# A hybrid diffusion layer on Trainium2: the two latent FFNs done in two phases, gate and up by seven products of half blocks

## The chip, the cores and the metric

The kernel runs on one core of one Trainium2 chip, as one program. The metric is the device time of one execution in microseconds (us). The engines work side by side, each on its own queue in order: TensorE (PE in the rows) multiplies, VectorE (DVE), ScalarE (ACT) and GpSimd (POOL) do the rest, and SyncE (SP) issues nearly all transfers between DRAM and SBUF.

## What is computed

One layer over 1024 latent tokens of width 1024 and 256 context tokens: a half-step FFN, a mixing sublayer, a second half-step FFN. The FFNs of the latent tokens are what changes:

```python
def rms_norm(x, g):
    return x * lax.rsqrt(jnp.mean(x * x, axis=-1, keepdims=True) + EPS) * g
def macaron_ffn(x, mod3, norm_pre, norm_post, w_gate, w_up, w_down):
    h = modulate(rms_norm(x, norm_pre), mod3[:, 0], mod3[:, 1])     # h * (1 + scale) + shift
    y = (jax.nn.silu(h @ w_gate) * (h @ w_up)) @ w_down             # 1024 -> 2816 -> 1024
    return x + 0.5 * mod3[:, 2] * rms_norm(y, norm_post)
...
mod = silu(c) @ ada_w + ada_b        # nine vectors of 1024: shift, scale, gate of each sublayer
h @ w_in  ->  u_f, z, x|B|C, dt      # mixing: Fourier group and a two-way SSD scan, then w_out
```

## The kernel before

Matrix products run in a 32-bit format that keeps part of a float32's digits, so each operand is split into a high and a low part (`split`, L182: ScalarE casts, VectorE subtracts) and each product is three matmuls (`mm3`, L398: high by high, high by low, low by high), 128 rows deep and at most 512 columns wide.

The hidden width 2816 is 22 tiles f of 128, taken in pairs j. `ffn_x` (L467) goes through the eleven pairs: gate and up of two tiles over all tokens (`g1_pair`, 8 row blocks x 2 chunks of 512 tokens x 3 matmuls, that is 48 for gate and 48 for up of a tile), then down (`g2`): for each of the 8 token tiles 12 matmuls into PSUM, which VectorE adds to the tile's y in SBUF (L465). With the last pair each token tile goes on to `post`: the norm of y, gate and residual (`post_norm`, L611), x1 written to DRAM, and the norm and the transposes (`ptr`, L642) of the next sublayer. In TensorE's queue the first products of the next sublayer (`pch`) stand among these. FFN1 begins with the first half of the tokens while the second half of x is loaded.

The modulations that FFN1 does not need itself are 14 units (`ada_units`, L541; a unit is half a vector): four loads of 512 KB (`adaR`), two steps on VectorE for each (L561, L563; twice as many where the context has the vector too), then a product with a matrix of ones (`pmod`) and a turn of the result. All 14 run beside FFN1, with a ring of three buffers.

`project` (L730) then does the channels of the Fourier group and C (`pch`, 256 columns), convolutions over the tokens (`conv`), the tokens' z and dt (`pz`), and the other channels (`pch`, 512 columns, 285 matmuls before anything else comes between). SBUF is cut by hand into regions (R, X, F); PSUM is cut anew for each stage. Which instruction comes when in a queue is set when the program is built; the queues are then fixed.

Of the kernel before, what the change touches and what calls it, by code (L numbers as in the profile page):

```python
# [26 lines left out]
R_WORDS, X_WORDS, F_WORDS = 20992, 13824, 18300  # L27

# columns of the per-partition vector table
# [6 lines left out]
# columns of the constant table  # L36
# [4 lines left out]
class Bank:  # L41
    """One SBUF tile cut by hand: an area is free again for what is traced after its release."""

    def __init__(self, pool, n, dtype, name):
        self.t = pool.tile([128, n], dtype, name=name)
        self.name = name
        self.view = {dtype: self.t}
        other = F32 if dtype is FR else FR
        self.view[other] = self.t.bitcast(other)
        self.holes = [(0, n)]  # L50


class Mem:
    """float32 areas and areas of float32r operands: a tile holds one kind only"""
# [67 lines left out]
class Kernel:  # L122
    def __init__(self, tc, a, out, st, dbg):
# [4 lines left out]
        self.xpool = None  # L128
# [3 lines left out]
        self.rs = self.nc.gpsimd  # the engine of the small steps of the norms  # L132
# [4 lines left out]
        self.swap(FR)  # L137

    def swap(self, kind):
        """the exchange region begins anew, with areas of one kind"""  # L140
        if self.xpool is not None:
            old = next(k for k, b in self.m.banks.items() if self.X in b)
            assert self.X.holes == [(0, X_WORDS)], self.X.holes
            self.m.banks[old].remove(self.X)
            self.xpool.close()
        self.xpool = self.st.enter_context(contextlib.ExitStack())
        self.nx = getattr(self, "nx", 0) + 1
        pool = self.xpool.enter_context(self.tc.tile_pool(name=f"x{self.nx}", bufs=1, reuse_waits="tile"))
        self.X = Bank(pool, X_WORDS, kind, f"X{self.nx}")
        self.m.banks[kind].append(self.X)  # L150

# [30 lines left out]
    def split(self, hi, lo, src, n, off=0, soff=None, E=None):  # L182
        """src (float32 area) into float32r parts hi + lo, exactly."""
# [47 lines left out]
    def run(self):  # L231
        m = self.m
        self.setup()
        self.banks(main=2, AUX=4)
# [7 lines left out]
    def setup(self):  # L242
# [5 lines left out]
        self.AB = m.alloc(8 * 2 * 5)  # (vector, shift|scale, d tile)  # L248
# [3 lines left out]
        self.cvec = m.alloc(16)  # L252
        self.ccols = m.alloc(256)
        self.G_d = self.dram([4, 1024], "G_d")

    def start(self):
        """norm of x, the shift and scale of its first sublayer, h^T."""
        m, nc, a = self.m, self.nc, self.a
        V, S = nc.vector, nc.scalar
        self.hh = [m.alloc(4096, FR, self.R0) for _ in range(2)]  # L260
        self.hl = [m.alloc(4096, FR, self.R0) for _ in range(2)]
        ada = Ring(m, 2048, 2)
        adaw = []

        def ada_load(j):
            if j < 8:
                adaw.append(ada.next())
                self.load(adaw[j], a["ada01"][j])

        xt = [m.alloc(1024) for _ in range(8)]  # L270
        junk = m.alloc(1024, FR, self.X)

        def xload(t):
            self.load(xt[t], a["x"][t * 128 : t * 128 + 128, :])
# [3 lines left out]
        xload(0)  # L278
        xload(1)
        self.load(self.pvt, a["pv"])  # L280
        ada_load(0)
        xload(2)
        xload(3)
        self.wrings(2, 3, self.X)
        self.raw.i = 0
        w1 = a["ffn1_w1"]
        self.wfirst = [self.weights(w1[0])]
        self.load(self.ct, a["consts"][:, :C_ID], 0, C_ID)
        ada_load(1)
        self.wfirst.append(self.weights(w1[1]))  # L290
        # silu(c), silu(c_ctx) as two columns of a 32-wide stationary operand
# [6 lines left out]
        V.tensor_copy(out=m.r(self.tri_r, 0, 256), in_=m.f(self.ct, C_TGT, C_TGT + 256))  # L298
        V.tensor_tensor(out=m.r(self.tri_r, 256, 384), in0=self.cst(C_TLE), in1=self.cst(C_TGT), op=ALU.add)

        full = Ring(m, 512, 2)
        ssm = m.alloc(256, top=True)

        def xnorm(t):
            ss = self.tmp(1)
            self.sumsq(m.f(xt[t]), ss, junk)
            self.rs = V if t < 4 and t % 2 == 0 else nc.gpsimd
            r = self.rstd(ss, 1, 1.0 / D)
            V.tensor_scalar(out=m.f(xt[t]), in0=m.f(xt[t]), scalar1=r, scalar2=None, op0=ALU.mult)

        def mods(j):
            w = adaw[j]
            P = self.psum("pada", "AUX")
# [4 lines left out]
            ada_load(j + 2)  # L318
# [9 lines left out]
        def hT(c, k):  # L328
            P = self.psum("ptr", "AUX")
            for t in range(4):  # L330
                nc.tensor.transpose(out=P[:, 128 * t : 128 * t + 128], in_=m.f(xt[4 * c + t], 128 * k, 128 * k + 128), identity=self.ident())
            f = full.next()
            if c and k % 2:
                S.activation(out=m.f(f), in_=P, func=AF.Identity, scale=self.A(0, k), bias=self.B(0, k))
            else:
                V.tensor_scalar(out=m.f(f), in0=P, scalar1=self.A(0, k), scalar2=self.B(0, k), op0=ALU.mult, op1=ALU.add)
            self.split(self.hh[c], self.hl[c], f, 512, k * 512, 0)

        for t in range(4):
            xnorm(t)  # L340
        P = [self.psum("gu"), self.psum("gu")]
        self.gfirst = P
        for j in range(8):
            mods(j)
            if 2 <= j < 6:
                # not before the loads that are needed sooner
                V.tensor_copy(out=m.f(xt[j + 2], 0, 1), in_=self.A(0, j))
                xload(j + 2)
                xnorm(j + 2)
            hT(0, j)  # L350
            for i in range(2):
                self.g_half_k(P[i], self.wfirst[i], (self.hh, self.hl, 512), 0, j)

        ada.release()
        self.yfirst = [m.alloc(1024) for _ in range(4)]

        def second():
            """the second half of the tokens, once the first has begun"""
            for k in range(8):
                hT(1, k)  # L360
            m.free(*xt, ssm, junk, self.ccols, self.cvec)
            self.banks(main=3, aux=1)
            full.release()
            self.raw.areas.append(m.alloc(1024, F32, self.F0))

        self.second = second

    # index of a vector: 0 x ffn1, 1 ctx ffn1, 2 x mix, 3 ctx mix, 4 x ffn2
# [29 lines left out]
    def mm3(self, outs, lh, ll, rh, rl, first, last):  # L398
        """outs[c] += (lh + ll)^T (rh[c] + rl[c]) but for the product of the two low parts"""
        n = len(outs)  # L400
        for ps, (l, r) in enumerate(((lh, rh), (lh, rl), (ll, rh))):
            for c in range(n):
                self.nc.tensor.matmul(out=outs[c], lhsT=l, rhs=r[c], start=first and ps == 0, stop=last and ps == 2)  # L403
# [11 lines left out]
    def g1_pair(self, w, hT, g):  # L415
        m, nc = self.m, self.nc
        P = self.psum("gate")
        self.g_half(P, [P[:, 0:512], P[:, 512:1024]], w, 0, hT, (0, 1))
        s = self.sg.next()
        nc.scalar.activation(out=m.f(s), in_=P, func=AF.Silu)  # L420
        P = self.psum("up")
        self.g_half(P, [P[:, 0:512], P[:, 512:1024]], w, 1, hT, (0, 1))
        nc.vector.tensor_tensor(out=m.f(s), in0=P, in1=m.f(s), op=ALU.mult)  # L423
        self.split(g[0], g[1], s, 1024)
# [13 lines left out]
    def g1_one(self, w, hT, g, c, P=None, off=0, n=None):  # L438
        """one chunk of at most 512 tokens, or n of it: gate and up in one PSUM tile"""
# [27 lines left out]
    def ffn_x(self, name, hT, y, post, step=lambda: None, first=None, gu=None, begun=lambda: None, tail=lambda i: None, ending=lambda: None):  # L467
        """all tokens; the first and the last two tiles of d_ff take the two halves of the tokens in turn.
# [11 lines left out]
        for j in range(NG):  # L480
# [10 lines left out]
            if last:  # L491
                ending()
# [1027 lines left out]
```

## Time and profile before

| what | value |
|---|---|
| median of 3 runs (lowest, highest) | 2373.26 us (2372.77, 2375.87) |
| the profiled execution, its span | 2374.1 us |
| TensorE busy | 2241.8 us, 94% |
| VectorE, ScalarE, GpSimd busy | 1230.7, 735.0, 438.6 us |
| FFN1 with the start, to the first z product | 0 to 868.4 us |
| project, context and mixing | 868.4 to 1628.2 us |
| FFN2 | 1628.2 to 2374.1 us |

The stages are read from the timeline of TensorE by the names of its products. A busy share is an average; where TensorE waits is read from the timeline and from the chain of waits.

### The profile page before, as it was taken

What the parts mean: (1) busy time and instruction counts of PE and PEld (TensorE: products, weight loads), DVE (VectorE), ACT (ScalarE), POOL (GpSimd) and SP (SyncE); (2) the same over time, 40 slices, a digit from 0 to 9 for tenths busy, and PEclk for the clock granted to TensorE, in tenths of its full rate; (3) what the DMA queues carried; (4) which work ended last, traced back from release to release, by engine and by line L of the source; (5) the groups of instructions that cost most, each with busy time, mean ns of one, the idle gap of its engine ahead of it and who ended that gap; (6) DMA issues with size and microseconds to landing.
All of it is one profiled execution on the core that took longest, in us unless ns stands there. A gap on an engine that the chain in (4) does not pass through costs nothing. (4 is left out here: it accounts for less than half of the span.)

```text
span 2374.1 us, 27935 instructions
## 1 busy us (share of the span) xinstructions
PE 2241.8 (94%) x11228; PEld 1898.4 (80%) x11228; DVE 1230.7 (52%) x1785; ACT 735.0 (31%) x1141; POOL 438.6 (18%) x490
## 2 busy tenths in 40 slices
PE   7999999999999999988989987898999999999997
PEld 4788888888888899877888866676888888888886
DVE  5744456555534732357888857785233332333335
ACT  3411111111113742336555554455311111111112
POOL 2000000000002500027775722662000000000005
PEclk9999999999999999998999989989999999999999
DMA  7322223333321421123445354333111111111104
GB/s 291 117 82 86 63 88 107 107 114 102 96 71 63 168 88 60 45 62 107 142 143 172 109 185 138 133 127 133 62 45 48 42 54 54 45 54 45 54 9 142
DMA packets 69009, 228.67 MB, mean 96 GB/s; under 512 B 8064, under 2 KB 13824, under 8 KB 67856
## 3 DMA queue, kind: packets, MB, share of 16 engines
q1 hardware_dynamic: 68880, 226.89, 29.3%
q8 instruction: 88, 1.44, 0.2%
q14 instruction: 41, 0.34, 0.0%
HBM read 200.37 MB, written 26.49 MB: 96 GB/s over the span
## 5 line engine op out<-in xcount | busy, mean ns | idle before, releaser
L403 PE MATMUL y<-X,R 128*128 128x512 f32 x2112 | 493.4, 391 | 6.6 <-ACT R L186 3.5
L403 PEld LDWEIGHTS y<-X,R 128*128 128x128 f32 x2112 | 396.1, 188 | 93.0 <-DVE F L465 5.9
L186 ACT CAST X<-F 128x1024 fp32r<-128x1024 f32 (+2 forms) x151 | 157.0, 1041 | 907.3 <-PE up L403 316.5
L403 PE MATMUL up<-R,X 128*128 128x512 f32 x1728 | 397.8, 389 | 0.0
L403 PE MATMUL gate<-R,X 128*128 128x512 f32 x1728 | 397.7, 389 | 0.0
L403 PEld LDWEIGHTS up<-R,X 128*128 128x128 f32 x1728 | 324.4, 188 | 67.3
L403 PEld LDWEIGHTS gate<-R,X 128*128 128x128 f32 x1728 | 324.4, 188 | 67.3
L187 DVE TENSOR_TENSOR X<-F,X 128x1024 fp32r<-128x1024 f32 (+2 forms) x150 | 183.6, 1226 | 300.4 <-ACT X L186 278.8
L195 POOL TENSOR_SCALAR F<-F 128x1 f32<-128x1 f32 x24 | 6.6, 275 | 1419.6 <-ACT F L216 1376.8
L465 DVE TENSOR_TENSOR F<-y,F 128x1024 f32<-128x1024 f32 x160 | 191.6, 1219 | 111.7 <-PE y L403 111.2
L187 DVE TENSOR_TENSOR R<-F,R 128x1024 fp32r<-128x1024 f32 (+3 forms) x167 | 190.0, 1141 | 99.5 <-ACT R L186 93.2
L186 ACT CAST R<-F 128x1024 fp32r<-128x1024 f32 (+4 forms) x184 | 159.0, 872 | 187.3 <-PE pch L403 48.1
L423 DVE TENSOR_TENSOR F<-up,F 128x1024 f32<-128x1024 f32 x36 | 44.1, 1225 | 299.6 <-PE up L403 299.6
L403 PE MATMUL gu<-R,X 128*128 128x512 f32 (+1 forms) x960 | 189.9, 355 | 5.0 <-DVE R L187 3.1
L403 PEld LDWEIGHTS gu<-R,X 128*128 128x128 f32 x960 | 156.6, 192 | 31.6 <-DVE R L187 5.3
L403 PE MATMUL pch<-R 128*128 128x512 f32 (+1 forms) x720 | 145.4, 360 | 7.6 <-DVE F L727 6.2
L403 PE MATMUL gu<-R 128*128 128x256 f32 x1056 | 142.8, 295 | 7.5 <-DVE X L465 6.2
L403 PEld LDWEIGHTS gu<-R 128*128 128x128 f32 x1056 | 135.8, 199 | 12.7 <-DVE X L465 7.4
L403 PEld LDWEIGHTS pch<-R 128*128 128x128 f32 x720 | 121.5, 193 | 27.7 <-DVE F L727 5.3
L1018 POOL TENSOR_TENSOR R<-F 128x384 fp32r<-128x384 f32 x128 | 128.7, 1033 | 35.4 <-PE pD L1052 20.0
L563 DVE SCALAR_TENSOR_TENSOR F<-F 128x512 f32<-128x512 f32 x140 | 101.5, 747 | 34.5 <-DMA F<-adaR 33.3
L403 PE MATMUL y<-R 128*128 128x512 f32 x264 | 73.0, 421 | 1.9 <-ACT R L186 1.9
(256 smaller groups left out, 2314.8 us busy)
## 6 DMA issues: line engine op xcount, KB each, us to landing
F<-ffn_w SPq DMA_DIRECT2D x132, 512.0 KB
F<-ffn_wd SPq DMA_DIRECT2D x66, 512.0 KB
F<-adaR SPq DMA_DIRECT2D x56, 512.0 KB
F<-w_ch SPq DMA_DIRECT2D x26, 512.0 KB
F<-x SPq DMA_DIRECT2D x16, 512.0 KB
F<-ada SPq DMA_DIRECT2D x8, 1024.0 KB
x_d<-F SPq DMA_DIRECT2D x16, 512.0 KB
F<-x_d SPq DMA_DIRECT2D x16, 512.0 KB
```

Of the source, the lines that this page charges most:

```text
L186: nc.scalar.copy(out=m.r(hi, off, off + n), in_=m.f(src, soff, soff + n))
L187: (E or nc.vector).tensor_tensor(out=m.r(lo, off, off + n), in0=m.f(src, soff, soff + n), in1=m.f(hi, off, off + n), op=ALU.subtract)
L195: V.tensor_scalar(out=mv, in0=ss, scalar1=scale * RSQ_M, scalar2=EPS * RSQ_M, op0=ALU.mult, op1=ALU.add)
L403: self.nc.tensor.matmul(out=outs[c], lhsT=l, rhs=r[c], start=first and ps == 0, stop=last and ps == 2)
L423: nc.vector.tensor_tensor(out=m.f(s), in0=P, in1=m.f(s), op=ALU.mult)
L465: nc.vector.tensor_tensor(out=m.f(y[t]), in0=P, in1=m.f(y[t]), op=ALU.add)
L563: V.scalar_tensor_tensor(out=ac, in0=m.f(w, 512 * i, 512 * i + 512), scalar=m.f(self.sil, 8 * v + k, 8 * v + k + 1), in1=ac, op0=ALU.mult, ...
L1018: G.tensor_tensor(out=m.r(R, 384 * i, 384 * i + 384).rearrange("p (h l) -> p h l", h=3), in0=self.cst(tri).unsqueeze(1).broadcast_to([128, ...
```

## The change

**Phase 1, gate and up.** The four quarters of the product are rows of two halves: two f tiles of a pair (columns of w), two halves of the 1024 rows of w (h), two halves of the tokens. Instead of eight products of quarters seven are done (`PROD`), on sums of quarters of w and of h. A unit u = (j, part) is gate or up of a pair: 7 products x 4 row steps x 3 = 84 matmuls of 512 columns where 96 were. VectorE makes the sums of weights (`usums`), low parts (`usplit`) and combines the results (`u_first`, `u_mid`, `u_late`, `u_end`). Sums of h are made once per FFN, in four steps (`h_sums`, `h_split`; GpSimd takes part of the lows). FFN1 needs all of x for them; FFN2 does its first pair plainly (192 matmuls), and reads h back from DRAM (`h3_d`) for the sums. Rows of g go to DRAM (`g_d`).

**Phase 2, down.** `ffn_down` goes three times over all f, for token tiles (0,1), (2,3,4), (5,6,7); y stays in PSUM. For each pass and f it loads and splits 512 KB of w and 128 or 192 KB of g. `post` takes y from PSUM; in FFN1 it goes through one buffer b.

**Modulations.** Units 0 to 5 stay beside FFN1 (ring of one), 6 to 13 go beside the z products (ring of two, one fp32 `pmod` each).

```diff
+PROD = {1: ("A11", "B11"), 2: ("A12", "B21"), 3: ("S4", "B22"), 4: ("A22", "T4"), 5: ("S1", "T1"), 6: ("S2", "T2"), 7: ("S3", "T3")}
...
+    def h_sums(self, hb):
+        b = [m.f(hb, 512 * q, 512 * q + 512) for q in range(7)]
+        V.tensor_tensor(out=b[4], in0=b[2], in1=b[3], op=ALU.add)
+        V.tensor_tensor(out=b[3], in0=b[3], in1=b[0], op=ALU.subtract)
+        V.scalar_tensor_tensor(out=b[5], in0=b[2], scalar=-1.0, in1=b[3], op0=ALU.mult, op1=ALU.subtract)
+        V.tensor_tensor(out=b[6], in0=b[1], in1=b[5], op=ALU.add)
...
+    def ffn_up(self, begun, step=lambda: None):
+        for u in range(n):
+            if u or not begun:
+                for p in (1, 6):
+                    self.product(u, p)
+            self.u_first(u)
...
+            if u + 1 < n:
+                self.usums(u + 1)
+                self.usplit(u + 1, "A11")
+            step()
+            if u > (1 if begun else 0):
+                self.u_late(u - 1)
+                self.usplit(u, "S4")
+            for p in (5, 7):
+                self.product(u, p)
+            self.u_mid(u)
+            if u + 1 < n:
+                self.usplit(u + 1, "S1")
+                if u + 2 < n:
+                    self.uload(u + 2)
+            step()
+        self.u_late(n - 1)
...
+        def prep(q):
+            p, f = todo[q]
+            t0, n = passes[p][0] * 128, len(passes[p]) * 128
+            w, g = self.wraw.next(), self.graw.next()
+            self.load(w, wd[f // 2][:, f % 2 * 1024 : f % 2 * 1024 + 1024])
+            self.load(g, self.g_d[f][:, t0 : t0 + n], 0, n)
+            wh, wl = self.wring.next()
+            gh, gl = self.gring.next()
+            self.split(gh, gl, g, n)
+            self.split(wh, wl, w, 1024)
...
+        ring, acc, sp = Ring(m, 1024, 1, F32, X2), Ring(m, 512, 2, F32, X2), Ring(m, 1024, 1, FR, X1)
+        st = self.ada_steps(self.ada_units(ring, acc, sp, (V,)), range(6))
+        self.ffn_up(True, lambda: next(st))
...
         zs = Ring(m, 384, 2)
+        ring, ac2 = Ring(m, 1024, 2, F32, self.Q), Ring(m, 512, 2, F32, self.Q)
+        st = self.ada_steps(self.ada_units(ring, ac2, None, (V,), "TR"), range(6, 14))
         for nm, n in (("w_zdt", 408), ("w_z1", 384)):
             for t in range(8):
                 P = self.psum("pz", "PZ")
                 self.tok_proj(P, n, t, sets[nm])
+                for _ in range(3):
+                    next(st)
```

Three places in the queues. First TensorE at the end of FFN1 (y: down, ptr: transposes of the normed tile, pch: first products of project), before:

```order
L403 MATMUL y<-X_65,R_60 128x512
L403 MATMUL pch<-R_60,X_65 128x256 x16
L403 MATMUL y<-X_65,R_60 128x512 x4
L403 MATMUL pch<-R_60,X_65 128x256 x4
L403 MATMUL y<-X_65,R_60 128x512 x14
L403 MATMUL pch<-R_60,X_65 128x256 x3
L642 MATMUL ptr<-F_61 128x128 x4
L403 MATMUL pch<-R_60,X_65 128x256 x4
L642 MATMUL ptr<-F_61 128x128 x4
L403 MATMUL pch<-R_60,X_65 128x256 x69
```

and now:

```order
L461 MATMUL y<-Q1a 128x512 x8
L461 MATMUL y<-Q1a,X3a 128x512 x4
L461 MATMUL y<-Q1a 128x512 x2
L803 MATMUL ptr<-F_61 128x128 x24
L461 MATMUL pch<-R_60 128x256 x48
L461 MATMUL pch<-R_60,X3a 128x256 x96
```

The transposes of three token tiles now stand in one row ahead of every pch. Second, TensorE at the end of the z products (pdec and ptot belong to the decays, pmod to the modulations), before:

```order
L403 MATMUL pz<-X_65,R_60 128x384 x73
L881 MATMUL pdec<-F_61 128x96
L882 MATMUL pdec<-F_61 128x96
L883 MATMUL pdec<-F_61 128x96
L884 MATMUL pdec<-F_61 128x96
L885 MATMUL ptot<-F_61,R_60 128x192
L403 MATMUL pz<-X_65,R_60 128x384 x119
L403 MATMUL pch<-R_60 128x512 x285
```

and now:

```order
L725 MATMUL pmod<-Q4a,R_60 128x512
L461 MATMUL pz<-X3a,R_60 128x384 x80
L725 MATMUL pmod<-Q4a,R_60 128x512
L1082 MATMUL pdec<-Q4a,F_61 128x96
L1083 MATMUL pdec<-Q4a,F_61 128x96
L1084 MATMUL pdec<-Q4a,F_61 128x96
L1085 MATMUL pdec<-Q4a,F_61 128x96
L1086 MATMUL ptot<-Q4a,R_60 128x192
L725 MATMUL pmod<-Q4a,R_60 128x512 x4
L461 MATMUL pch<-R_60 128x512 x285
```

Four products of modulations stand between the last z product and the first pch. Third, SP's queue at the same place, now (z_d: z written out, grows and G_d: the gate rows of units 12 and 13):

```order
L990 DMA z_d<-Q4a 128x384
L184 DMA Q4a<-adaR 128x1024 x11
L736 DMA Q4a<-grows 1x1024
L184 DMA Q4a<-adaR 128x1024
L741 DMA G_d<-Q4a 1x512
L184 DMA Q4a<-adaR 128x1024 x3
L736 DMA Q4a<-grows 1x1024
L741 DMA G_d<-Q4a 1x512
L184 DMA Q4a<-ctx 128x1024 x2
```

Fifteen loads of modulation weights stand behind the last z written out; before, none stood there.

## Rows read from the trace of the kernel before

**Rows 1.** Page: span, and busy time of each engine (share of span, instructions).

```profile
span 2374.1 us, 27935 instructions
...
PE 2241.8 (94%) x11228; PEld 1898.4 (80%) x11228; DVE 1230.7 (52%) x1785; ACT 735.0 (31%) x1141; POOL 438.6 (18%) x490
```

**Rows 2.** Chain of waits in FFN2: start us, us, engine and work.

```profile
1834.64 10.88 PE gate L403 x48
...
1878.16 21.76 PE y L403 x96
```

**Rows 3.** Stretches: busy us of each engine, clock, DMA share, GB/s.

```profile
core 0: us, PE busy (x) PEld busy (x) DVE busy (x) ACT busy (x) POOL busy (x), PEclk, DMA share, GB/s
...
100.00:400.00 300.00, 299.82 (x1320) 247.09 (x1319) 159.86 (x195) 59.04 (x63) 0.00 (x0) 1.00 0.27 84
```

**Rows 4.** TensorE by line up to 89.02 us: busy us, mean ns, idle.

```profile
L403 PE MATMUL gu<-R,X 128*128 128x512 f32 x145 | 41.0, 424 | 5.0 <-DVE R L187 3.1 <-ACT R L186 1.5 <-DVE X L187 0.4
...
L403 PE MATMUL y<-X,R 128*128 128x512 f32 x24 | 6.4, 410 | 0.0
```

**Rows 5.** Timeline of TensorE, end of FFN1's start.

```profile
89.02 11.04 PE L403 MATMUL gu<-R,X 128*128 128x512 f32 x48
```

**Rows 6.** Groups by line and form of VectorE, ScalarE and GpSimd: mean ns of one.

```profile
L187 DVE TENSOR_TENSOR X<-F,X 128x1024 fp32r<-128x1024 f32 x144 | 178.0, 1237 | 276.8 <-ACT X L186 276.4 <-PE gu L403 0.3
...
L563 DVE SCALAR_TENSOR_TENSOR F<-F 128x512 f32<-128x512 f32 x140 | 101.5, 747 | 34.5 <-DMA F<-adaR 33.3
...
L187 DVE TENSOR_TENSOR R<-F,R 128x512 fp32r<-128x512 f32 x28 | 19.7, 712 | 11.3 <-ACT R L186 11.3
...
L186 ACT CAST X<-F 128x1024 fp32r<-128x1024 f32 x145 | 152.0, 1050 | 905.8 <-PE up L403 316.5 <-PE y L403 281.4 <-PE gate L403 266.3
...
L187 POOL TENSOR_TENSOR R<-F,R 128x1024 fp32r<-128x1024 f32 x17 | 43.5, 2562 | 19.8 <-ACT R L186 19.8
```

**Rows 7.** Timeline of VectorE and GpSimd near the end.

```profile
2325.53 1.28 DVE L619 SCALAR_TENSOR_TENSOR F<-F 128x1024 f32<-128x1024 f32 x1 [1.05 <-POOL F L202]
...
2328.80 2.40 POOL L620 TENSOR_TENSOR F<-F 128x1024 f32<-128x1024 f32 x1
...
2328.88 3.40 DVE L619 SCALAR_TENSOR_TENSOR F<-F 128x1024 f32<-128x1024 f32 x1 [2.06 <-POOL F L202]
```

**Rows 8.** Timeline of SP's queue and of VectorE: a load of modulation weights.

```profile
94.73 1.09 SPq L172 DMA_DIRECT2D F<-adaR  x2
...
98.43 1.41 DVE L563 SCALAR_TENSOR_TENSOR F<-F 128x512 f32<-128x512 f32 x2 [2.97 <-DMA F<-adaR]
...
100.90 1.41 DVE L563 SCALAR_TENSOR_TENSOR F<-F 128x512 f32<-128x512 f32 x2
```

**Rows 9.** Timeline of TensorE in project: channel and z products.

```profile
857.80 10.72 PE L403 MATMUL pch<-R,X 128*128 128x256 f32 x88
...
868.36 2.40 PE L403 MATMUL pz<-R 128*128 128x408 f32 x12
...
939.23 64.87 PE L403 MATMUL pch<-R 128*128 128x512 f32 x285 [0.63 <-ACT F L789]
```

**Rows 10.** Timeline of ScalarE: silu of the last convolution.

```profile
880.09 1.06 ACT L728 ACTIVATE F<-F 128x1024 f32<-128x1024 f32 x1 [2.13 <-DVE F L727]
```

**Rows 11.** Timeline of TensorE: start and end of FFN2.

```profile
1628.19 8.10 PE L403 MATMUL gu<-R,X 128*128 128x512 f32 x35
...
1646.47 1.12 PE L642 MATMUL ptr<-F 128*128 128x128 f32 x4 [2.01 <-ACT F L647]
...
1647.24 24.20 PE L403 MATMUL gu<-R,X 128*128 128x512 f32 x96
...
2352.42 8.35 PE L403 MATMUL y<-X,R 128*128 128x512 f32 x36
```

**Rows 12.** Chain of waits: a transfer of 384 KB.

```profile
1485.13 3.65 DMA F<-y_d
```

**Rows 13.** Stretch (busy, clock, DMA) and timeline of TensorE after an idle spell.

```profile
1095.00:1100.00 5.00, 0.18 (x1) 0.50 0.20 50
...
1100.92 3.62 PE L403 MATMUL y<-R 128*128 128x512 f32 x8
```

More of the change, by code (lines that the diff above doesn't have):

```diff
@@ L258, in start @@
         m, nc, a = self.m, self.nc, self.a
[L259 to L274, printed above, removed]
+        V, S, G = nc.vector, nc.scalar, nc.gpsimd
@@ L280, in start @@
         self.load(self.pvt, a["pv"])
         ada_load(0)
[L282 to L288, printed above, removed]
-        ada_load(1)
-        self.wfirst.append(self.weights(w1[1]))
+        for t in range(4, 8):
+            self.load(xt[t], a["x"][t * 128 : t * 128 + 128, :])
+        ada_load(1)
+        self.raw = Ring(m, 2560, 1, F32, self.F0)
@@ L357, in second @@
[L357 to L366, printed above, removed]
+            o = m.f(hb, 512 * slot, 512 * slot + 512)
+            if c:
+                S.activation(out=o, in_=P, func=AF.Identity, scale=self.A(0, k), bias=self.B(0, k))
+            else:
+                V.tensor_scalar(out=o, in0=P, scalar1=self.A(0, k), scalar2=self.B(0, k), op0=ALU.mult, op1=ALU.add)
@@ L402, in mm3 @@
             for c in range(n):
-                self.nc.tensor.matmul(out=outs[c], lhsT=l, rhs=r[c], start=first and ps == 0, stop=last and ps == 2)
+                self.nc.tensor.matmul(out=outs[c], lhsT=l, rhs=r[c], start=first and ps == 0, stop=last and ps == 2, skip_group_check=again)
     def g_half(self, P, outs, w, half, hT, chunks):
@@ L541, in ada_units, with units, uload @@
-    def ada_units(self):
+    def units(self, name, j0):
+        self.uw, self.ulist = self.a[name + "_w1"], [(j, part) for j in range(j0, NG) for part in range(2)]
+        self.uraw, self.P, self.srow, self.U = {}, {}, {}, {}
+    def uload(self, u):
+        j, part = self.ulist[u]
+        m = self.m
+        w = self.uraw[u] = self.raw.next()
+        self.nc.sync.dma_start(out=m.f(w, 0, 2048).rearrange("p (f c) -> p f c", f=2),
+                               in_=self.uw[2 * j : 2 * j + 2, :, 1024 * part : 1024 * part + 1024].rearrange("f p c -> p f c"))
@@ new lines, in u_first, with u_dest @@
+    def u_first(self, u):
+        self.U[u] = self.ut.next()
+        U = self.m.f(self.U[u])
+        self.nc.scalar.copy(out=U, in_=self.P[u, "A"])
+        self.nc.vector.tensor_tensor(out=U, in0=self.P[u, "B"], in1=U, op=ALU.add)
+    def u_dest(self, u):
+        j, part = self.ulist[u]
+        if part == 0 and j not in self.srow:
+            self.srow[j] = (self.sg.next(), self.sg.next())
+        m = self.m
+        s = [m.sub(self.srow[j][q // 2], 512 * (q % 2), 512) for q in range(4)]
+        return s, (s if part == 0 else [None] + self.cc)
@@ new lines, in u_late @@
+    def u_late(self, u):
+        m, nc = self.m, self.nc
+        V = nc.vector
+        j, part = self.ulist[u]
+        s, d = self.u_dest(u)
+        self.product(u, 2)
+        self.u_end(u, 0, s, d)
+        for p, tag, q in ((3, "C", 1), (4, "D", 2)):
+            self.product(u, p)
+            V.tensor_tensor(out=m.f(d[q]), in0=self.P[u, tag], in1=m.f(self.U[u]), op=ALU.add)
+            self.u_end(u, q, s, d)
+        if part:
+            for i in range(2):
+                nc.sync.dma_start(out=self.g_d[2 * j + 1 - i], in_=m.f(self.srow[j][i]))
@@ L597, in unit, with ada_steps @@
                                                op0=ALU.add, op1=ALU.mult)
-        def done():
-            for r in (ring, acc, sp):
-                r.release()
-        return unit, done
+        return unit
+    @staticmethod
+    def ada_steps(unit, us):
+        for u in us:
+            yield from unit(u)
+        while True:
+            yield
     def gload(self, slot):
@@ new lines, in ffn1, with step, post @@
+        self.wch = []
+        def step(p):
+            state["n"] = state.get("n", 0) + 1
+            i = len(self.wch)
+            if p == 2 and i < 6 and state["n"] >= 46 + 3 * i:
+                w, r = state["w"][i], self.wraw.next()
+                self.load(r, a["w_ch"][i])
+                self.split(w[0], w[1], r, 1024)
+                self.wch.append(w)
+        def post(t, P):
+            self.rs = V if t > 5 else nc.gpsimd
+            c = t // 4
+            b, xx = state["b"], x.next()
+            self.post_norm(P, m.f(b), state["G"], xx, a["x"][t * 128 : t * 128 + 128, :], V)
+            nc.sync.dma_start(out=self.x1_d[t], in_=m.f(b))
+            self.pre_norm(m.f(b), 2, m.r(self.hh[c]), m.r(self.hl[c]), 512, (t % 4) * 128, xx, full, "AUX", True, V if t > 6 else None)
@@ new lines, in ffn1, with pairs @@
+        state["b"] = m.alloc(1024, F32, X2)
+        self.ffn_down("ffn1", ((0, 1), (2, 3, 4), (5, 6, 7)), post, step, before)
+        for r in (x, full, self.graw, self.wraw):
+            r.release()
+        m.free(state["G"], state["b"])
+        for r in (self.wring, self.gring):
+            for q in r.areas:
+                m.free(*q)
+    def pairs(self, bank, nw, ng):
+        m = self.m
+        if bank is self.Q:
+            self.wring, self.gring = Pairs(), Pairs()
+        self.wring.areas += [tuple(m.alloc(1024, FR, bank) for _ in range(2)) for _ in range(nw)]
+        self.gring.areas += [tuple(m.alloc(384, FR, bank) for _ in range(2)) for _ in range(ng)]
```

585 lines of the change are left out of this document (368 added, 217 removed).

## The prediction

> **What bounds the kernel now.** I read the busy shares first: TensorE works 2241.8 of 2374.1 us [rows 1], so only work that it loses, or waits that it gains, can change the time. The chain of waits then gives the price of a product: in the FFNs it is nothing but matmuls, 48 in 10.88 us and 96 in 21.76, so a 512-column matmul costs 0.2267 us [rows 2]. The table of stretches shows what stands beside it: in 100:400 TensorE has no gap while VectorE is busy 159.86 of 300 us [rows 3]. VectorE therefore has about 47% to give in the FFNs, no more. The profiled execution (span 2374.1) is 0.8 us above the median of 2373.26, so I sum against 2374.1 and take 0.8 off. Changes within 0.2% (4.7 us) I call the same.
>
> **The change part by part.**
>
> *Fewer products.* Each latent FFN had 22 x (96 + 48) = 3168 matmuls of 512 columns. FFN1 now has 22 units of 84 and 1056 for down = 2904, FFN2 192 plain ones, 20 x 84 and 1056 = 2928. 504 x 0.2267 = -114.3 us, if TensorE never waits: -59.9 and -54.4. The 16 matmuls that the modulations lose in FFN1 are another -3.7.
>
> *Start of FFN1.* At 89.02 us the old kernel had done 144 gate/up and 24 down matmuls [rows 4, 5], worth 38.1 us: 51 us lost. The new one needs all of x, and for each of four steps sums of the quarters of h before its products. For a step VectorE has four sums (0.71 each) and a low part of 2048 (2 x 1.24), together 5.3 us, so 21 us; with the scaling of eight x tiles, eight evictions and modulations, and the sums and lows of the first weights I count some 47 us [rows 6]. GpSimd takes the other lows, four of 1536, 1.5 x 2.56 = 3.84 us each [rows 6]. While it works on SBUF, a VectorE operation with two SBUF inputs stands: the same line took 1.28 us alone and 3.40 beside a GpSimd addition of 2.40 [rows 7]. So 47 + 15 us, from about 18 us on: the last low at 80 us, 39 matmuls before it. That is 74 us lost with a few waits, +23. If the two engines do not meet, +8; if every wait adds, +30.
>
> *FFN1, gate and up.* A unit gives TensorE 19.04 us. VectorE has three sums and three lows of weights, an addition and four combinations, four multiplications more for up: 10.8 us for gate, 13.6 for up [rows 6]. In 16 or so of 22 units a modulation adds up to twelve steps of 0.75 [rows 6], which makes 20 to 22 us; the units between have slack, but not all of it carries over. I take +10, between 0 and +45 (no carry at all).
>
> *Up to down.* The first g rows are loaded only after the last ones have left their buffers. FFN1: two VectorE operations, a write (I take the 3.65 us of a 384 KB transfer [rows 12]), a load, a cast: 10 us idle. FFN2: 6 us. After an idle spell the granted clock read 0.50, and 8 matmuls took 3.62 us where 1.81 is the full rate [rows 13], so 2 to 3 us each time: +12 and +9. Between passes: post runs through one buffer b; I find 5 and 3 us.
>
> *Tail of FFN1.* Ahead, TensorE's queue had the channel products (pch) between y and the transposes; now 24 transposes, those of tiles 5, 6 and 7, stand before the first pch, so all pch wait for tile 7. A turn of b is two passes of 1024 (2 x 1.24), a 512 KB write and the issue, about 7.5 us; two turns and the norm of tile 7 end some 20 us after the last y; with the clock 22. What was lost there before: from 89.02 to the first pz at 868.36 are 779.3 us [rows 5, 9], of which 3000 matmuls take 680, 40 of the modulations 9 and 576 pch at 10.72/88 us 70 [rows 9]. The other 20 are 64 transposes (I take 6) and waits of 14. So +8.
>
> FFN1 together: -59.9 - 3.7 + 23 + 10 + 12 + 5 + 8 = -6.
>
> *Eight modulations beside the z products.* This is where I expect the gain to go. Units 6 to 13 ran under FFN1, where their loads were hidden. Now they share two buffers in project, and their last four products stand in TensorE's queue ahead of 285 pch which need nothing of them. One load of 512 KB: two issued at 94.73, the first used at 98.43, so 3.7 us, then two steps, 1.41 [rows 8]; with 0.2 for the issue a buffer turns in 5.3 us. A unit has four loads on two buffers, 10.6 us, then its fp32 product (between 0.23 and 1 us, I take 0.7) and a turn of the same ring for its result (1.7): 13 us, and units hardly overlap, since the result holds a buffer. Four units also write a row to DRAM before the buffer is free, +2 each. The first load goes out after the last convolution, whose silu ended at 881.15, 12.8 us after the first pz [rows 9, 10]; later ones queue on SP behind the z weights, whose raw buffers now overlap the convolution's input: +5. And pz products themselves wait: z_d writes and pmods are in the same queues, some +6. So 12.8 + 8 x 13 + 8 + 5 + 6 = 136 us from the end of the first pch to the next; it was 939.23 - 868.36 = 70.9 [rows 9]. +65. Lower bound: the loads alone keep both buffers turning, 12.8 + 32 x 5.3 / 2 = 98, +27. Upper: +80.
>
> The load's price has a rule beside it: the Trainium skill (DMA: Bandwidth & Descriptors, Anatomy of one DMA) gives 2.0 us plus bytes at 436 GB/s for a DMA. By that a load is an estimated 3.2 us, 0.5 less than the row, a unit 1.0 less, and the stage some 8 us shorter; it was fitted on another issuing path, and I keep the row.
>
> *FFN2.* 144 plain matmuls cover 33 us after the transposes of tile 7, with the clock 35. Meanwhile h goes to DRAM and comes back for the sums: write 4, two loads in line 8, sums and lows 10, the same again for the other two steps 15, first weights 5, their sum and cast 2.5: 44 us. +10 idle, +12 with the clock (0 to +20). Up to down +9, passes +3. Before, of 2374.1 - 1628 = 746 us the products took 718; 28 were lost, of which 8 at the transposes remain [rows 11]. The last pair's 7 us go, and the end after the last y is some 10.5 instead of 13.3, as no addition to y is left: -9.5. FFN2: -54.4 + 12 + 9 + 3 - 9.5 = -40.
>
> The mixing stages between keep their operations; h goes to DRAM on a queue with room. 0, +-8.
>
> **Sum.** -6 + 65 - 40 = +19; 2374.1 + 19 - 0.8 = 2392. That is slower by 0.8%.
>
> **Rivals.**
> (a) Faster. The modulations stream: if the results turn over while the next loads run, the stage costs the lower bound, +27, and the sum is 2354. For it: VectorE has little else there. Against: a unit's second load waits for the buffer that holds the last result. It decides as soon as a unit takes less than 13 - 19/8, about 10.6 us.
> (b) Slower still: VectorE becomes the bound in FFN1. Each unit with modulation steps then takes the 22 us of its VectorE work, and nothing carries over: +45 instead of +10, 2427. For it: single loads into a ring of one, which VectorE waits for in order. Against: units without steps have 5 us of slack.
> (c) The passes are bound by loads: w is read three times, in pass 0 640 KB for every 2.72 us of matmuls. With three raw buffers a turn is 3.6 us, a cast 1.05 and a low 1.24 [rows 6], 6.2 with issue, 2.1 per f, so it fits; if loads lengthen to 6 us under this rate, 44 f lose 0.2 to 0.6 each, about 20: 2412.
> (d) The change does not do what it says, if the 84 matmuls ran at another rate than 0.2267. They have the shapes of before; only waits could show it, and these are (b).
>
> **How the numbers follow.** Forecast 0.55, own range 2365 to 2425; (a) 0.23, 2330 to 2370; (b) 0.12; (c) 0.10. The terms add up in doubt to some 30 us: start -15/+7, up -10/+35, project -38/+15, FFN2 +-10. 2392 is the likeliest. Range 2345 to 2432: it leaves out the lower third of (a) and the top of (b). Faster by over 0.2% (below 2368.5): 0.19 of (a) and 0.04 of the forecast, 0.23. Same: 0.03 and 0.06, 0.09. Slower: 0.68.
>
> **What would show it.** In the new profile: pch of 512 columns start about 136 us after the last pch of 256, with TensorE idle four times for some 12 us, ended by modulation steps of VectorE; a gap of 10 us between the last product of up and the first y in FFN1 and of 6 in FFN2; 20 us between the last y of FFN1 and the first pch; 10 us after the last plain gate/up of FFN2; the last low of h near 80 us. The FFNs between gaps should show 84 matmuls in 19.04 us. I am wrong if the gap before pch is below 25 us, or if the units of FFN1 take more than 21 us on average.

## The result, and the profile after

The changed kernel takes 2432.94 us (2430.91 to 2435.34), the kernel before 2374.2 us: a ratio of 1.0249, interval 1.0234 to 1.0263. It is 58.7 us slower; I had forecast 19 us slower, and the time is 0.9 us above my range. The profiled execution has a span of 2428.4 us against 2374.1 [rows 1], so 54.3 us are to be placed.

The page: span, and busy time of each engine.

```profile
span 2428.4 us, 28213 instructions
PE 2173.6 (90%) x10532; PEld 1810.0 (75%) x10532; DVE 1507.0 (62%) x2216; ACT 918.7 (38%) x1393; POOL 428.2 (18%) x446
```

TensorE has 68 us less work than before and 54 us more span. By the four stretches that the prediction used (their ends are starts of TensorE's rows, here and in [rows 9, 11]):

| stretch | before | after | forecast | measured |
|---|---|---|---|---|
| FFN1, to the first z product | 868.36 | 879.34 | -6 | +11.0 |
| first z product to the first pch of 512 | 70.9 | 160.1 | +65 | +89.2 |
| mixing, to the first gate/up of FFN2 | 689.0 | 667.8 | 0 | -21.2 |
| FFN2, to the end | 745.9 | 721.2 | -40 | -24.7 |
| sum | | | +19 | +54.3 |

**Start of FFN1**, where [rows 5] stood before. Timeline of VectorE, GpSimd and TensorE (start us, us, engine, line, what; in brackets the idle time before it and what ended it).

```profile
32.45 3.56 POOL L422 TENSOR_TENSOR R<-F,R 128x1536 fp32r<-128x1536 f32 x1 [32.01 <-ACT R L416]
32.97 3.59 DVE L396 TENSOR_TENSOR F<-F 128x512 f32<-128x512 f32 x1
...
75.88 2.72 DVE L716 TENSOR_SCALAR X3b<-X3b,F 128x512 f32<-128x512 f32 x2 [3.39 <-DMA X3b<-adaR]
78.52 0.68 DVE L396 TENSOR_TENSOR F<-F 128x512 f32<-128x512 f32 x1
...
84.57 0.80 PE L461 MATMUL pb<-X3a,Q1a 128*128 128x512 f32 x1 [5.86 <-ACT X3a L416]
88.89 1.22 PE L461 MATMUL pb<-X3a,Q1a 128*128 128x512 f32 x2 [2.67 <-DVE X3a L422]
```

The reader is to see two things. A sum of 512 columns took 3.59 us beside a low part of GpSimd and 0.68 us alone. And ahead of the sums of the last step VectorE stood 3.39 us for a load of a modulation, which nobody needed yet: the scheduler had put it there. TensorE got the last low part at 88.89, with 42 products done.

**Gate and up.** Stretches: us, busy time of the engines, clock, DMA share, GB/s; the third one lies in the down passes.

```profile
100.00:300.00 200.00, 200.00 (x872) 163.36 (x871) 154.44 (x201) 58.66 (x70) 0.00 (x0) 1.00 0.33 108
300.00:500.00 200.00, 200.00 (x872) 163.35 (x871) 146.62 (x197) 58.35 (x69) 0.00 (x0) 1.00 0.34 111
560.00:680.00 120.00, 119.73 (x531) 97.89 (x529) 62.77 (x73) 58.41 (x87) 21.42 (x45) 1.00 0.66 208
```

TensorE has no gap, at the full clock, and VectorE has a quarter of the time left. But 872 matmuls in 200 us are 0.2294 us each, not 0.2267 [rows 2]; a few of these are modulation products. The timeline of TensorE in FFN2 says it better:

```profile
1871.04 2.97 PE L461 MATMUL pc<-R,X7a 128*128 128x512 f32 x12
...
1882.21 2.92 PE L461 MATMUL pa<-R 128*128 128x512 f32 x12
```

Between these two starts stand 48 matmuls: 11.17 us, 0.2327 each, where 48 took 10.88 before. Nothing waits here. Over the whole trace, the start-to-start times of the matmuls of 512 columns (those below 0.26 us) add up to some 23 us above 0.2267 us each; in the kernel before to some 2.5.

**Down and the tail of FFN1.** Timeline of TensorE.

```profile
523.55 6.73 PE L461 MATMUL y<-Q1a 128*128 128x512 f32 x16 [12.02 <-ACT Q1a L198]
...
700.23 1.97 PE L803 MATMUL ptr<-F 128*128 128x128 f32 x8 [6.67 <-ACT F L793]
...
785.50 0.61 PE L461 MATMUL y<-Q1a 128*128 128x512 f32 x2
792.61 1.97 PE L803 MATMUL ptr<-F 128*128 128x128 f32 x8 [6.49 <-ACT F L793]
800.79 1.97 PE L803 MATMUL ptr<-F 128*128 128x128 f32 x8 [6.21 <-ACT F L793]
808.19 1.97 PE L803 MATMUL ptr<-F 128*128 128x128 f32 x8 [5.44 <-ACT F L793]
809.81 7.36 PE L461 MATMUL pch<-R 128*128 128x256 f32 x48
```

12 us between up and down, and 24 us from the last y to the first pch, with the transposes of the three tiles 8.2 and 7.4 us apart; the forecast had 12 and 22 with the clock. The 6.67 us at 700.23 are the same chain inside a pass: transposes stand in the queue ahead of y and wait for the norm.

**Modulations beside the z products**, against [rows 9]. Timeline of TensorE.

```profile
879.34 4.63 PE L461 MATMUL pz<-R 128*128 128x408 f32 x24
895.28 6.05 PE L461 MATMUL pz<-R 128*128 128x408 f32 x24 [11.32 <-ACT R L198]
...
915.94 1.02 PE L725 MATMUL pmod<-Q4a,R 128*128 128x512 f32 x2
...
1006.48 2.05 PE L725 MATMUL pmod<-Q4a,R 128*128 128x512 f32 x2 [12.87 <-DVE Q4a L718]
1021.23 2.04 PE L725 MATMUL pmod<-Q4a,R 128*128 128x512 f32 x2 [12.70 <-DVE Q4a L718]
1038.36 2.04 PE L725 MATMUL pmod<-Q4a,R 128*128 128x512 f32 x2 [15.09 <-DVE Q4a L718]
1039.41 66.25 PE L461 MATMUL pch<-R 128*128 128x512 f32 x285
```

Four gaps of 11 to 15 us, the last four units, ended by modulation steps of VectorE: the picture that I had drawn, only longer. The first product came 36.6 us after the first z product, and the others every 17.5 us on average: 19 to 20 beside the z products, 14.8 to 17.6 behind them. Why so long is seen in the timeline of SP's queue and VectorE (the first row is the first load of the stage):

```profile
898.64 0.33 SPq L184 DMA_DIRECT2D Q4a<-adaR  x1
...
954.96 0.33 SPq L184 DMA_DIRECT2D Q4a<-adaR  x1
958.96 0.48 DVE L716 TENSOR_SCALAR Q4a<-Q4a,F 128x512 f32<-128x512 f32 x1 [4.03 <-DMA Q4a<-adaR]
960.26 1.66 SPq L184 DMA_DIRECT2D Q4a<-adaR  x2
966.40 3.11 DVE L718 SCALAR_TENSOR_TENSOR Q4a<-Q4a,F 128x512 f32<-128x512 f32 x4 [4.65 <-DMA Q4a<-adaR]
967.97 0.33 SPq L184 DMA_DIRECT2D Q4a<-adaR  x1
972.32 1.54 DVE L718 SCALAR_TENSOR_TENSOR Q4a<-Q4a,F 128x512 f32<-128x512 f32 x2 [2.80 <-DMA Q4a<-adaR]
973.88 0.33 SPq L184 DMA_DIRECT2D Q4a<-adaR  x1
977.92 0.49 DVE L716 TENSOR_SCALAR Q4a<-Q4a,F 128x512 f32<-128x512 f32 x1 [4.07 <-DMA Q4a<-adaR]
```

Loads go out at 954.96, 960.26 (two), 967.97 and 973.88, where the next unit begins: three turns for four loads, each of them issued only when VectorE has used what lay in the buffer before, and used 4.0 to 6 us later. One of the two at 960.26 went out at 961.58 in fact, when the result of the unit before had left its buffer. A unit takes five places of the ring, four loads and its result. With two buffers the result lies between the last load of one unit and the first of the next, so that both of these fall on the same buffer and cannot overlap.

**FFN2.** Timeline of TensorE (for [rows 11]).

```profile
1707.22 0.73 PE L461 MATMUL gu<-R 128*128 128x512 f32 x2 [1.22 <-ACT R L198]
...
1771.77 1.22 PE L461 MATMUL pc<-Q8a,R 128*128 128x512 f32 x2 [11.82 <-ACT R L198]
...
2172.09 8.62 PE L461 MATMUL y<-Q8a 128*128 128x512 f32 x24 [8.25 <-ACT Q8a L198]
...
2404.56 12.45 PE L461 MATMUL y<-X7a 128*128 128x512 f32 x54
```

The bubble ahead of the products (11.82 against 10 us idle), the one ahead of down (8.25 against 6) and the end (2428.4 less 2417.0, 11.4 against 10.5) are near their forecasts.

### The profile page after: what moved, and what is told of

Same layout as the page of the kernel before. It is cut to its first block, busy times and chain, and to the rows that moved or that the text cites. A ratio compares the mean times of both kernels' runs of the same rounds, so it can differ in the third digit from the quotient of the medians.

```text
span 2428.4 us, 28213 instructions
## 1 busy us (share of the span) xinstructions
PE 2173.6 (90%) x10532; PEld 1810.0 (75%) x10532; DVE 1507.0 (62%) x2216; ACT 918.7 (38%) x1393; POOL 428.2 (18%) x446
## 5 line engine op out<-in xcount | busy, mean ns | idle before, releaser
L198 ACT CAST R<-F 128x1024 fp32r<-128x1024 f32 (+2 forms) x135 | 139.9, 1039 | 224.8 <-PE pd L461 68.9
L198 ACT CAST Q1a<-F 128x1024 fp32r<-128x1024 f32 (+1 forms) x115 | 129.8, 1131 | 221.0 <-PE pd L461 126.4
L199 DVE TENSOR_TENSOR R<-F,R 128x1024 fp32r<-128x1024 f32 (+1 forms) x117 | 155.3, 1330 | 59.8 <-ACT R L198 52.5
L461 PE MATMUL gu<-R 128*128 128x256 f32 (+1 forms) x1152 | 164.7, 302 | 5.4 <-DVE X5a L512 1.9
L461 PE MATMUL y<-Q1a 128*128 128x512 f32 x564 | 138.8, 399 | 12.0 <-ACT Q1a L198 12.0
L461 PEld LDWEIGHTS y<-Q1a 128*128 128x128 f32 x564 | 109.0, 194 | 36.6 <-ACT Q1a L198 12.5
L199 DVE TENSOR_TENSOR Q1a<-F,Q1a 128x1024 fp32r<-128x1024 f32 x93 | 114.6, 1233 | 32.0 <-ACT Q1a L198 30.9
L461 PE MATMUL y<-X7a 128*128 128x512 f32 x534 | 124.1, 390 | 0.0
L461 PEld LDWEIGHTS y<-X7a 128*128 128x128 f32 x534 | 100.2, 188 | 21.6
L461 PE MATMUL pa<-R,Q1a 128*128 128x512 f32 x330 | 93.4, 399 | 0.0
L461 PEld LDWEIGHTS y<-Q8a 128*128 128x128 f32 x348 | 67.3, 194 | 23.6 <-ACT Q8a L198 8.7
```

Source lines behind the costliest of these rows:

```text
L198: nc.scalar.copy(out=m.r(hi, off, off + n), in_=m.f(src, soff, soff + n))
L199: (E or nc.vector).tensor_tensor(out=m.r(lo, off, off + n), in0=m.f(src, soff, soff + n), in1=m.f(hi, off, off + n), op=ALU.subtract)
```

## The experiments

Ratios are to the kernel before, each with its interval.

**The rate of the matmuls.** Nothing waits, so either the shape of a product or the place of its operands makes a matmul 3% longer. The diff cuts SBUF into other regions; the exchange region, which holds half of the operands, begins at byte 174048 of a partition, the others at 16512 and 140928. Before, it began at 173696. I first aligned it to 64 bytes:

```
-R_WORDS, Q_WORDS, X_WORDS, F_WORDS = 20992, 8192, 13824, 10108
+R_WORDS, Q_WORDS, X_WORDS, F_WORDS = 20992, 8192, 13832, 10108
```

(with 8 words more in the last part of each cut of the region).

> The changed kernel with 8 words more in the exchange region, so that its tiles start at a multiple of 64 bytes as the others do (before they start 32 bytes off); nothing else. Theory A: a matmul of 512 columns takes 0.2267 us where its moving and its stationary operand have the same address modulo 64 bytes, and about 0.234 where these differ by 32; 2174 of the 6992 such matmuls differ, so the units of 84 matmuls go from 19.51 to 19.04 us and the kernel gets 17 to 25 us faster, 2410 to 2416 us. Theory B: the units are slow because a product of 12 matmuls changes its PSUM bank; then 19.51 stays and the time is 2433.

Measured: 2429.23 us, 1.0231 (1.0216 to 1.0246), and the sum above 0.2267 is some 22 us. Theory A, in the form with 64 bytes, is wrong. At the same time I shifted the region of the kernel before by 32 bytes, with a larger region below it:

```
-R_WORDS, X_WORDS, F_WORDS = 20992, 13824, 18300
+R_WORDS, X_WORDS, F_WORDS = 20992, 13824, 18308
```

> The kernel before, with 8 words more in the region that lies below the exchange region, so that the latter starts 32 bytes off a multiple of 64 bytes; nothing else. Theory A (operands apart by 32 bytes modulo 64): 6408 matmuls of 512 columns take 0.234 instead of 0.2267 us, so about 47 us slower, 2421 us. Theory B (changes of the PSUM bank): 2374 us, no change.

Measured: 2410.93 us, 1.0156 (1.0138 to 1.0173). The chain of waits shows every 48 matmuls at 11.20 us, 0.2333 each:

```profile
1722.41 11.20 PE gate L403 x48
1733.62 11.20 PE up L403 x48
```

The channel products, whose operands both lie in one region (R), kept their rate in the same run: 285 of them in 64.92 us, against 64.87 [rows 9]. Timeline of TensorE:

```profile
957.96 64.92 PE L403 MATMUL pch<-R 128*128 128x512 f32 x285 [0.63 <-ACT F L789]
```

So place alone does it, with the same products and the same order (in this run 321 of TensorE's 11228 rows between 1472 and 1638 us stand elsewhere, in the shifts below none); only the period was wrong. Next, 88 words more for the exchange region of the changed kernel, which puts it where it was before, and a shift of 64 bytes in the kernel before (`F_WORDS` 18316):

```
-R_WORDS, Q_WORDS, X_WORDS, F_WORDS = 20992, 8192, 13824, 10108
+R_WORDS, Q_WORDS, X_WORDS, F_WORDS = 20992, 8192, 13912, 10108
```

> The changed kernel with 88 words more in the exchange region, so that all operand tiles of TensorE start at the same address modulo 512 bytes, as in the kernel before (in the changed kernel they differ by 160 or 352, in the run padded to 64 bytes by 192 or 320); nothing else. Theory A2: the rate depends on that difference over a longer period than 64 bytes; then the units of 84 matmuls take 19.04 us, the sum above 0.2267 us per matmul (23 us in the changed kernel) is nearly gone, and the time is about 2410 us. Theory B: the changes of PSUM bank in a unit make it; then the units stay at 19.5 us and the time at 2430 us, whatever the addresses.

> The kernel before, with the exchange region shifted by 64 bytes instead of 32. If a difference modulo 64 bytes alone counted, its matmuls are back at 0.2267 us and the time is 2374 us. If the period is longer (theory A2), they stay at about 0.233 us and the time is near 2410 us.

Measured: 2414.84 us, 1.0169 (1.0154 to 1.0184), for the first, 18 us less than the change, with TensorE's products in the same order; the sum above 0.2267 fell from some 23 to less than 2 us, and the matmuls of a unit are back at their old rate. Timeline of TensorE in that run: 60 matmuls in 13.60 us.

```profile
1859.76 2.88 PE L461 MATMUL pa<-R,X7a 128*128 128x512 f32 x12
...
1873.36 2.88 PE L461 MATMUL pa<-R 128*128 128x512 f32 x12
```

The second: 2410.18 us, 1.0141 (1.0118 to 1.0163), gate and up at 0.2333. Theory A2 holds, and theory B falls. Two more shifts of the kernel before (`F_WORDS` 18332 and 18364) were to find the period:

> The kernel before, with the exchange region shifted by 128 bytes (32 words) instead of 32 or 64 bytes. It asks how long the period of the address effect is. If only the difference modulo 128 bytes counts, the gate and up matmuls are back at 0.2267 us and the time is 2374 us; if the period is 256 or 512 bytes, they stay at about 0.233 us and the time near 2410 us.

> The same with a shift of 256 bytes (64 words). If the period is 256 bytes or less, 0.2267 us and 2374 us; if it is 512 bytes, about 0.233 us and 2410 us.

Measured: 2411.83 us, 1.015 (1.0133 to 1.0167), with 128 bytes, and 2374.57 us, 0.9996 (0.9987 to 1.0006), with 256. The period is 256 bytes. In the last one, the chain of waits:

```profile
1703.79 10.88 PE gate L403 x48
```

**The modulations.** Four more buffers in their ring:

```
 ring, ac2 = Ring(m, 1024, 2, F32, self.Q), Ring(m, 512, 2, F32, self.Q)
+ring.areas += [m.alloc(1024) for _ in range(4)]
```

> The changed kernel with six load buffers instead of two for the eight modulations beside the z products. Theory C: the stage from the first z product to the first channel product of 512 columns (160 us) is long because the loads of a unit wait for the two buffers; with six it falls to about 90 us (eight units of about 9 us of VectorE work after 13 us), and the kernel gets about 70 us faster, 2363 us. Rival D: the order of the products in TensorE's queue and VectorE's own work set the 15 us of a unit; then the stage stays at 140 us or more and the time is above 2413 us. If the 21 us that the mixing stages behind it won came from work that the long stage hid, some of them are given back: 2363 becomes up to 2384 us.

Measured: 2371.74 us, 0.9993 (0.9983 to 1.0002): one line takes the loss back. The stage is 101.6 us, near the 98 of my lower bound and short of the 90 of theory C, which gets 61 of its 70 us; D falls. Two things are not parted here: with the buffers 137 of TensorE's 10532 products also changed their places in the queue, and a ring of two without the fifth use (the result elsewhere) was not run. The mixing stages stay at 665 us, so what they won was not work that the long stage had hidden. TensorE's timeline there:

```profile
878.42 4.63 PE L461 MATMUL pz<-R 128*128 128x408 f32 x24
893.82 6.41 PE L461 MATMUL pz<-R 128*128 128x408 f32 x24 [10.77 <-ACT R L198]
...
979.00 2.04 PE L725 MATMUL pmod<-Q4a,R 128*128 128x512 f32 x2 [2.07 <-DVE Q4a L718]
980.05 20.32 PE L461 MATMUL pch<-R 128*128 128x512 f32 x81
```

**The start of FFN1.** The load buffer of its modulations goes to memory that the quarters of h hold:

```
+ring = Ring(m, 1024, 1, F32, F0)
 self.ut = Ring(m, 512, 2, F32, F0)
-self.cc = [m.alloc(512, F32, F0) for _ in range(3)]
+self.cc = [m.alloc(512, F32, F0 if i == 2 else X2) for i in range(3)]
...
```

> The changed kernel with the load buffer of FFN1's modulations in memory that the quarters of h hold until their last low part is made (two column buffers take its old place), so that VectorE can't meet the first modulation step ahead of the last sums of h. Theory E: VectorE waited 3.4 us for that load and worked 4 us on modulations at 72 to 80 us while the sums of the last step stood behind; without this the last weights of h are used at about 81 instead of 88.9 us and the kernel gets 6 to 8 us faster, 2426 us. Rival F: the start is set by GpSimd's low parts beside VectorE; then the last product of the start stays near 88 us, and the time at 2433.

Measured: 2424.07 us, 1.021 (1.0193 to 1.0228), about 9 us less, but not where I had said. Timeline of TensorE:

```profile
79.45 0.79 PE L461 MATMUL pb<-X3a,Q1a 128*128 128x512 f32 x1 [1.54 <-ACT X3a L416]
...
89.80 0.73 PE L461 MATMUL pc<-R,Q1a 128*128 128x512 f32 x2 [3.06 <-ACT Q1a L198]
...
510.96 4.54 PE L461 MATMUL y<-Q1a 128*128 128x512 f32 x12 [2.49 <-ACT Q1a L198]
521.23 4.52 PE L461 MATMUL y<-Q1a 128*128 128x512 f32 x12 [5.73 <-ACT Q1a L198]
```

The last low part of h was ready at 81.7 instead of 88.8 us. Then the weights of the second unit were late, 3.06 us at 89.80, and up ended only 3.1 us earlier (508.1 against 511.1). The rest came from an accident of the layout: a buffer for loads of g moved away from the last rows of g, so that SP issued the first load of g at 507.62 us instead of 520.64, the first y began 2.9 us after up instead of 12.4, and a wait of 5.73 us followed. That also shows what the gap between up and down was: buffers, not the round trip of g as a whole. The first y's got earlier by 12.6 us, the last one by 8.3.

**Together.** Three of these edits (13912 words, six buffers, the late load):

> The changed kernel with three edits together: operand tiles at equal addresses modulo 512 bytes, six load buffers beside the z products, and the first modulation load behind the last low of h. If the three causes are independent: 2433 - 61 (six buffers) - 9 (late load) - 20 (addresses, theory A2) = about 2343 us, faster than the kernel before by 1.3%. By theory B: 2363 us.

Measured: 2353.58 us, 0.9912 (0.9897 to 0.9927), faster than before by 20 us where the sum of the single edits gives 26; 3 us of the rest are in the stage (104.2 against 101.6). Then two more, loads of z weights ahead of pch and more buffers for the norms:

```
+self.raw = Ring(m, 1024, 3, F32, self.F0)
+zw = [self.raw.next() for _ in range(3)]
+for q in range(3):
+    self.load(zw[q], a["w_zdt"][:, 816 * q : 816 * (q + 1)], 0, 816)
...
-x, full = Ring(m, 1024, 2, F32, F0), Ring(m, 512, 2, F32, X2)
+x, full = Ring(m, 1024, 3, F32, F0), Ring(m, 512, 2, F32, X2)
-state["b"] = m.alloc(1024, F32, X2)
+state["b"] = Ring(m, 1024, 2, F32, X2)
...
```

> The three edits and two more: the first three blocks of the z weights are loaded ahead of the channel products of 256 columns, into memory that the convolutions don't use (the z products waited 11.3 us for them), and the norms of FFN1's down passes have two buffers b and three x instead of one and two (TensorE waited 6.2 and 5.4 us for the second and third tile of the last pass). Theory: 9 us less in the first place and 6 in the second, some 15 us below the run with three edits, 2328 us. Rival: the z products then wait for modulation steps instead and the tail is bound by the chain of one tile; then it is within 5 us of that run.

Measured: 2342.68 us, 0.9865 (0.9846 to 0.9884), 11 us less than three edits, in other places than expected. From the first y of FFN1 to the last it takes 255.2 instead of 265.9 us: the second b ended the waits inside the passes. The tail keeps 22.6 of 23.6 us. The last z product stands 76.0 us behind the first instead of 89.3, but the stage stays at 104.1 us, because the last modulations end it, as the rival said. So in that ring the z weights did not set the length of the stage. Timeline of TensorE:

```profile
946.20 2.05 PE L725 MATMUL pmod<-Q4a,R 128*128 128x512 f32 x2 [12.85 <-DVE Q4a L718]
954.25 2.04 PE L725 MATMUL pmod<-Q4a,R 128*128 128x512 f32 x2 [6.00 <-DVE Q4a L718]
961.19 9.20 PE L461 MATMUL pch<-R 128*128 128x512 f32 x33 [4.89 <-ACT R L198]
```

So the modulations begin one stage earlier, with one step after each group of pch:

```
     S.copy(out=m.f(self.uc[i - 2], l, l + n), in_=P[:, 0:n])
+next(st)
...
-for _ in range(3):
+for _ in range(2):
     next(st)
```

(the ring and its first two buffers are set up ahead of that loop, seven more behind it).

> The run with five edits, and the eight modulations begun one place earlier: one step after each of the 24 groups of channel products of 256 columns (VectorE is busy there for 7 of 60 us), on two buffers and then nine, and two steps instead of three after each z product. In the run with five edits the last z product stands at 933 us and the channel products of 512 columns begin at 961 us behind the last modulations. Theory: modulations cost nothing where VectorE and the queue are idle and TensorE has other products ahead; the stage falls from 104 to about 78 us (384 z products in some 71 us and 8 fp32 products), 2342.7 - 26 = 2317 us. Rival: with two buffers their products stand in TensorE's queue ahead of channel products and wait there (13 to 15 us of loads for a unit against 14 us of five groups); then the 70 us of the channel products grow by what the stage loses, and the time stays within 8 us of 2343.

Measured: 2324.73 us, 0.9773 (0.9757 to 0.979), 20 us less than five edits by the times relative to before. The first pch of 512 columns starts at 938.96, 74.6 us after the first z product. The 256-column pch grew from 71.0 to 82.1 us: three of the products waited there, for 3.3 us and less. Both theories had a part of it, the first the larger.

At last, GpSimd's low parts in the start go to VectorE:

```
-(nc.gpsimd if o == 0 else nc.vector).tensor_tensor(
+nc.vector.tensor_tensor(
```

> The same kernel, and in the start of FFN1 the four low parts of 1536 that GpSimd makes go to VectorE. Theory G: beside a low part of GpSimd a VectorE operation with two SBUF inputs takes up to 3.6 instead of 0.69 us (some 9 us over the four steps); VectorE does the four low parts itself in 4 x 1.75 = 7 us, so the start moves by -2 us and the time by no more than 3 us. Rival: the blocking is what holds the start; then it is 9 us shorter.

Measured: 2309.04 us, 0.972 (0.9705 to 0.9734), another 16 us. The rival holds, and more than that: the last low part begins at 73.09 instead of 80.04 us, and up ends at 490.5 instead of 502.9. Stretches of that run show that TensorE, with shorter waits, has a granted clock of 0.97 in 0:60 instead of 0.83 in the run above (means of its two levels, 1 for 2.4 and 0.50 for 1.2 GHz). The run changes two things at once: nothing of GpSimd stands in VectorE's way, and the low part itself takes 1.75 instead of 3.56 us. It does not part them. Timeline of VectorE:

```profile
33.97 0.68 DVE L396 TENSOR_TENSOR F<-F 128x512 f32<-128x512 f32 x1
34.57 1.75 DVE L422 TENSOR_TENSOR R<-F,R 128x1536 fp32r<-128x1536 f32 x1
...
73.09 2.29 DVE L422 TENSOR_TENSOR X3a<-F,X3a 128x2048 fp32r<-128x2048 f32 x1 [1.97 <-ACT X3a L416]
```

This kernel has all products of the change and is 2.8% faster than the kernel before.

## Why the prediction was right in kind and wrong in size

**Right.** Slower, and because of the modulations in project, which eat more (+89.2) than the FFNs give (+11.0 and -24.7). The start waits for the low parts, and up to down and the tail cost within 3 us of what I had counted. With the operands in place FFN2 takes 710.4 us (1699.6 to 2410.0 in that run), 35.5 less than before, where I had -40.

**The step that failed first: "A unit has four loads on two buffers, 10.6 us, then its fp32 product ... and a turn of the same ring for its result ...: 13 us".** I let the two buffers turn side by side, two turns for four loads. With five uses a unit in a ring of two the loads took three turns, 17.5 us a unit: from the first product to the last, seven units later, it took 122.4 us, where 13 each, 6 for rows written and 6 for waits at pz make 103. Six buffers brought the stage from 160.1 to 101.6 us. The start of the stage was nearly right: its first load went out at 898.64, 19.3 us after the first z product, where I had 12.8 + 5. The single load took 4.0 us from issue at 954.96 to use at 958.96, so even my row of 3.7 was short. By the Trainium skill (DMA: Bandwidth & Descriptors, Anatomy of one DMA), whose fit is for transfers that GpSimd issues, it would be an estimated 3.2 us; the measurement decides.

**The second: rival (d), "they have the shapes of before; only waits could show it".** The 84 matmuls did run at another rate, and no wait showed it. The cause is the place of the operands, which the diff moves without a word. It is worth 18 us here, of which 5.7 lie in FFN1 and 10.8 in FFN2, by the starts of the stretches in the run with 13912 words.

**Terms mis-sized.** *Start*: 79 us lost instead of 74 (88.89 less 42 x 0.2267), with some 9 us of VectorE blocked by GpSimd, where I had 15, and a load of modulations ahead of the sums, which I had not. *VectorE in up*: 0 instead of +10; it was busy 154 of 200 us, and rival (b) fell. *Passes of FFN1*: from 523.55 to 786 stand 1056 y, 239.4 us; of the 23 us beyond, 3 are the clock after the gap (0.50, that is 1.2 GHz, up to 529) and some 4 transposes; the other 16 I had at 5. Some 2 of them are the place of the operands (from the first y to the last it took 259.8 instead of 262.2 us in the run with 13912 words), and the second b took 11 in its run. Rival (c) fell: with DMA at 208 GB/s TensorE was busy 119.73 of 120 us in 560:680. *Up to down in FFN1*: 12 idle and 16 matmuls in 6.73 instead of 3.63 us, 15 instead of 12.

**Open: the mixing stages.** They got 21 us shorter where I had none, and 16 to 25 us in every run with the change. TensorE's rows stand in another order there, and its idle times above 0.3 us sum to 63.6 instead of 80.8 us. It isn't work hidden by the long stage (the run with six buffers). Whether the new cut of memory or the scheduler's order did it was not tried. That the time lies only 0.9 us above my range is therefore luck: without these 21 us, which no term of the sum had, it would lie 22 above.

**Rival (a)** is what six buffers make true: modulations that stream, at 101.6 us. It needed another ring than the change has.

## What to carry to other kernels

When work is moved to another stage, count the ring places that one unit takes, results too, and write down which load falls on which buffer; the time of a unit followed from that here, not from the number of loads. After any new cut of SBUF compare the starts of TensorE's two operands modulo 256 bytes with those of before, and the start-to-start time of the matmuls in the trace: an offset cost 3% of the products of 512 columns here and shows as no wait. And in a start where TensorE waits for VectorE, look in VectorE's rows for a wait that belongs to later work, and for another engine that stands in its way.

## What the runs showed of the hardware

- In the kernel before a matmul of 512 columns in gate and up takes 0.2267 us, with its stationary and moving operands at the same address modulo 256 bytes, and a mean of 0.233 when one region is shifted by 32, 64 or 128 bytes. Shifted by 256 it is 0.2267 again. In the changed kernel 2174 products start at unequal addresses; from start to start they took a mean of 0.234 us and the others 0.228, so some with equal addresses were slow too. Why the addresses count no run shows. pch of 256 columns showed nothing of it: 96 from R and X3a, unequal, started in 11.27 us, 0.1174 each, and those from R alone at 0.120. The Trainium skill (SBUF — State Buffer, Who interferes with whom) has TensorE read its two operands through independent ports and wait for nobody; from that one would expect no address to matter. The measurement decides.
- A VectorE operation with two SBUF inputs that met a low part of GpSimd took 3.59 instead of 0.68 us; doing the low parts on VectorE was worth 16 us in all. The Trainium skill (SBUF — State Buffer, Who interferes with whom) says that such an operation contends with a GpSimd instruction that reads SBUF, and the trace agrees.
- An fp32 product of a modulation shows as two matmuls, 2.04 us together at the granted clock of 0.50 (1.2 GHz), after TensorE had been idle for 11 to 15 us, and 1.02 at 915.94 at the full clock (2.4 GHz), with z products just before.
